# The 32x32 blocks of a delta rule's inversion, taken to one matrix per partition on chip instead of through DRAM

## The chip, the cores and the metric

The kernel runs on one core of a Trainium2 chip. The metric is the device time of one execution in microseconds, smaller is better. Three executions were timed, and one more was recorded by the hardware profiler; its trace and its page are what this document reads.

## The reference, cut to what matters

The kernel computes one decoder layer for a sequence of 1024 tokens and a model width of 1024: a normalised input projection, two mixing branches (an RWKV-7 branch and an S5 branch), gates that merge them, an output projection and a convolutional feed-forward part. The change lies in the RWKV-7 branch, whose core is a scan with a state `S` of 64x64 for each of 8 heads:

```python
def wkv7_scan(r, decay, k, v, a_vec, b_vec):
    ...
    def step(S, inp):
        r_t, w_t, k_t, v_t, a_t, b_t = inp
        sa = jnp.einsum('bhij,bhj->bhi', S, a_t)
        S = (S * w_t[:, :, None, :] + sa[..., None] * b_t[:, :, None, :]
             + v_t[..., None] * k_t[:, :, None, :])
        return S, jnp.einsum('bhij,bhj->bhi', S, r_t)
    ...
    _, ys = lax.scan(step, S0, xs)

def rwkv7_branch(p, mu, w0, w2, a0, a2, g2, k_k, k_a, r_k, lnx_w, lnx_b):
    ...
    y = wkv7_scan(rh, decay.reshape(hs), kh, vh, -kk, kk * ah)
    ...

# the merge: sigmoid(gA)*A + sigmoid(gB)*B, then one output projection
```

The kernel doesn't run this step by step. It takes chunks of 64 tokens. Within a chunk the term `sa` of a token depends on the tokens ahead of it through a strictly triangular 64x64 matrix, so a chunk needs the inverse of one unit triangular matrix per head. This inverse is what the change is about.

## The kernel before, in words

The sequence is worked in two halves of 512 tokens (`th` 0 and 1), each of 8 chunks. The 8 heads lie in two groups (`g`), each of two pairs (`u`) of two heads (`h`). For a half the steps are:

1. **Front** (`rwkv_front`): decays, scaled keys and the products of a group. At its end stand the gram matrices (L716 on PE, L720 masks them on DVE into `gr`), and a product for the bonus term (L724 into `pb`, L736 on DVE with `v`).
2. **Inversion** (`rwkv_inv`): each 64x64 triangular matrix is seen as two 32x32 diagonal blocks and one block beside them. For a half there are 2 groups x 2 blocks x 2 pairs x 8 chunks x 2 heads = 128 diagonal blocks. They are brought to one block per partition, so that one DVE instruction works on all of them, and 30 steps of two tensor_tensor instructions (L789 the product, L791 the sum) build the inverses. In the kernel before, the blocks go there through DRAM: L729 (eight DMAs a half, issued by POOL) writes them from `gr` to `md`, L777 reads `md` into `mt`, one block per partition. Afterwards L793 writes the inverses to `xd`, and eight DMAs at L798 bring them back into `gr`. The identity from which the inverse starts is written by two POOL memsets. A copy of one element (L783) from a result of `rwkv_nat` into the inverse's row 0 makes the inversion begin only after the transposes of nat.
3. **Nat** (`rwkv_nat`, L747): PE transposes of the keys, copied out by ACT (L754, L756, L767).
4. **Level** (`rwkv_level`): the block beside the diagonal, from the two inverses. DVE transposes the first diagonal block (L812), then come two rounds of 64 matmuls of 32x32 (L822 is the first) with ACT copies after each.
5. **Chain** (`rwkv_chain`): the eight chunks one after another, each in three steps (PE L879, ACT copy; PE L887, DVE copy L890; PE L902, DVE L903 and L904).
6. **Out** (`rwkv_out`): normalisation, bonus and gate.

These steps are small and depend on each other. PE's time between them is filled with large matrix products ("fill"): the input projection, the tiles of the two gates (`gate_tiles`, ACT L1158 takes each out of the PSUM tile `gm` and stores it), and then `merge`: gates of the first branch and GLU tiles, gates of the second branch (DVE L1203 multiplies a gate from DRAM with the PSUM tile), and the output projection. The tile `gm` has two slots in this part of the program, and the ring `ev`, into which gates are loaded, has three. A fill tile of 128x512 is a row of k-steps, each of three matmuls (L172, L173, L174) since every operand is split in a high and a low part; L156 (ACT) and L157 (DVE) split the weights, L226 and L227 the activations.

PE's order is written by the program itself: `drive` takes steps from lanes (two preparation lanes, the chain lane, the out lane) and one k-step of fill (`background`) whenever no lane is due. A lane says how long its step takes and how long it is to be left alone afterwards; T_MT, T_INV and T_INV2 are such numbers, for the time from the grams to nat and from nat to the level in the first and the second half. They decide how many k-steps of fill stand between two steps. The orders on DVE, ACT, POOL and SP are made by a scheduler from priorities (the inversion and the weights have the same high one, `HPW`), and each engine then runs its own order strictly.

Of the kernel before, what the change touches and what calls it, by code (L numbers as in the profile page):

```python
# [9 lines left out]
F32 = mybir.dt.float32  # L10
# [3 lines left out]
ALU = mybir.AluOpType  # L14
# [52 lines left out]
class Kern:  # L67
# [564 lines left out]
    def rwkv_tiles(self, d, g, th):  # L632
        pool = self.rk if g else self.rka
        d["ar"] = self.tg("ar", 1, (128, 2, 8, 128), pool=pool)
        d["bk"] = self.tg(f"bk{g}", 1, (128, 2, 8, 128), pool=self.rka)
        d["gr"] = self.tg("gr", 1, (128, 2, 8, 2, 128), pool=pool)
        d["V"] = self.tg(f"V{g}", 1, (128, 8, 2, 64))
        d["md"] = self.md[th][g]
        d["bv"] = self.dram.tile([2, 128, 512], F32, tag="bv", name=self.nm("bv"), bufs=3)

    def rwkv_front(self, d, g, th, pt, start):
# [3 lines left out]
        o = slice(th * 512, th * 512 + 512)  # L645
# [10 lines left out]
        for u in range(2):  # L656
            p = 2 * g + u
# [51 lines left out]
        for u, e in enumerate(L):  # L709
# [13 lines left out]
                    f["pb"] = self.rp()  # L723
                    mm(f["pb"], self.rkb[:, f["p"]], f["r"], start=True, stop=True)  # L724
# [34 lines left out]
    def nat_v(self, d, u, pv):  # L759
# [5 lines left out]
        for k, sl in enumerate(HALF):  # L765
            for h in range(2):
                self.nc.scalar.copy(to[HALF[1 - h], :, k], ps[sl, :, h])  # L767

    def rwkv_inv(self, ds, th):

        nc, V = self.nc, self.nc.vector
        mx = self.tg("mt", 1, (128, 2, 1024))
        mt, x = mx[:, 0], mx[:, 1]
        with self.tc.high_priority(HPW):
            nc.gpsimd.memset(x, 0.0)
            nc.gpsimd.memset(x[:, 0:1024:33], 1.0)
            nc.gpsimd.dma_start(mt, self.md[th].rearrange("g b e q t -> (g b e) (q t)"))  # L777
        yield 0, T_MT
        tie = self.rwkv_nat(ds[1], 1)
        yield 2.0, 0  # L780
        with self.tc.high_priority(HPW):
            mt, x2 = (t.rearrange("p (q t) -> p q t", t=32) for t in (mt, x))
            self.nc.scalar.copy(x2[:, 0, 1:2], tie[:, 0, 0:1])  # L783
            V.tensor_copy(x2[:, 0, 1:32], mt[:, 0, 1:32])
            for q in range(1, 31):
                n, m = q + 1, 31 - q
                tm = self.tg("tm", 1, (128, 256), pool=self.rka)
                tv = tm[:, :n * m].rearrange("p (s t) -> p s t", t=m)
                V.tensor_tensor(tv, x2[:, 0:n, q:q + 1].to_broadcast([128, n, m]),  # L789
                                mt[:, q:q + 1, q + 1:32].to_broadcast([128, n, m]), ALU.mult)  # L790
                V.tensor_tensor(x2[:, 0:n, q + 1:32], x2[:, 0:n, q + 1:32], tv, ALU.add)  # L791
            xds = self.dram.tile([2, 2, 32, 32, 32], F32, tag="xd", name=self.nm("xd"), bufs=2)
            nc.gpsimd.dma_start(xds.rearrange("g b e s t -> (g b e) (s t)"), x)  # L793
            for g, d in enumerate(ds):
                for blk in range(2):
                    for h in range(2):
                        o = 64 * h + 32 * blk
                        nc.gpsimd.dma_start(d["gr"][o:o + 32, :, :, h, 32 * blk:32 * blk + 32].rearrange("p u c t -> p (u c) t"),  # L798
                                            xds[g, blk].rearrange("(e h) s t -> h s e t", h=2)[h])

    def rwkv_level(self, ds):

# [1013 lines left out]
    def front_half(self):  # L1816
# [31 lines left out]
        with tc.tile_pool(name="rk", bufs=1) as self.rk, tc.tile_pool(name="evb", bufs=NEV) as self.evp, \  # L1848
                tc.tile_pool(name="psy", bufs=1, space=PSUM) as self.psx:
            self.ps, self.ngm = self.psx, 2  # L1850
            self.rwkv_setup()
            self.wfp = self.rk
            self.ds = [[{}, {}], [{}, {}]]
            self.grams = 0
            self.fronts, self.masked, self.preps, self.chains, self.chunks, self.outs, self.z = 0, 0, 0, 0, 0, 0, {}
            self.md = [self.dram.tile([2, 2, 32, 32, 32], F32, name=f"md{th}") for th in range(2)]
# [151 lines left out]
```

## Time and profile before

| | us |
|---|---|
| three timed executions | 1474.89, 1477.7, 1479.7 (median 1477.7) |
| the profiled execution | 1475.75 |
| its span in the trace | 1474.0 |
| idle time of PE from 480 to 640 us | 13.7 in all |
| the inversion's steps, first half | 351.04 to 376.86 |
| the inversion's steps, second half | 548.08 to 591.76 |

The mean granted clock of PE over this execution was 0.987. How to read the profile: PE, DVE, ACT and POOL are the tensor, vector, scalar and general engines, PEld is PE's weight load and SP the engine that issues most DMAs. A wait "PE gm L172 <- ACT ev L1158" is idle time of PE ahead of a matmul of line 172 that writes the tile `gm`, ended by an instruction of line 1158 on ACT that writes `ev`. A window's row gives busy time for each engine, and the clock that PE was granted, 1.00 being full speed. The DMAs that the change touches, with their size and the median time from issue to landing in us:

```profile
md<-gr POOLq DMA_DIRECT2D x16, 64.0 KB, 4.6
mt<-md POOLq DMA_DIRECT2D x2, 512.0 KB, 4.0
xd<-mt POOLq DMA_DIRECT2D x2, 512.0 KB, 5.2
gr<-xd POOLq DMA_DIRECT2D x16, 64.0 KB, 3.8
```

### The profile page before, as it was taken

The page shows a single profiled execution, that of the slowest core. Times are in us where ns is not written, and L with a number is a line of the kernel's source. Part 1 is how long each engine was busy: PE and PEld are TensorE (multiplying, and loading weights), DVE is VectorE, ACT ScalarE, POOL GpSimd, SP SyncE. Part 2 cuts the span into 40 slices and gives each one's busy share as a digit, 9 for nine tenths or more (in the row PEclk, how much of TensorE's full clock was granted, in tenths as well). Part 3 has the DMA queues.
Part 4 walks back from the last instruction along what each step waited for, and adds up shares of the span by engine and source line. Part 5 has one row for each costly group of instructions (what it writes and reads, how often), then busy time and mean ns, then how long its engine had stood idle before and what let it go on. Part 6 is the DMA issues. An engine that isn't in the chain of part 4 may idle for free. (4 is left out here: it accounts for less than half of the span.)

```text
span 1474.0 us, 24155 instructions
## 1 busy us (share of the span) xinstructions
PE 1420.3 (96%) x9284; PEld 1161.8 (79%) x9284; DVE 1072.4 (73%) x1761; ACT 729.6 (50%) x1167; POOL 58.9 (4%) x116
## 2 busy tenths in 40 slices
PE   7999999999999999899999999999999999999996
PEld 5778888788877777677788877888888887888775
DVE  8977775665425859657698798777777777697677
ACT  7677654443334653634455454444444544444441
POOL 0000000011100110100000000000000000000001
PEclk9999999999999999899999999999999999999998
DMA  6453433643511575633474543222222227934723
GB/s 219 116 194 120 134 96 88 206 123 117 171 62 63 170 238 164 187 124 108 142 223 145 192 136 112 82 86 86 86 86 86 73 71 256 341 123 140 243 75 114
DMA packets 121284, 206.26 MB, mean 140 GB/s; under 512 B 29248, under 2 KB 35520, under 8 KB 121168
## 3 DMA queue, kind: packets, MB, share of 16 engines
q1 hardware_dynamic: 113296, 182.43, 39.3%
q0 software_dynamic: 6144, 19.99, 4.0%
q10 hardware_dynamic: 1728, 2.29, 0.4%
q8 instruction: 73, 1.20, 0.3%
q14 instruction: 43, 0.35, 0.1%
HBM read 150.14 MB, written 52.43 MB: 137 GB/s over the span
## 5 line engine op out<-in xcount | busy, mean ns | idle before, releaser
L172 PE MATMUL gm<-hh,wh 128*128 128x512 f32 x672 | 276.4, 411 | 9.4 <-DVE ev L1203 4.1
L173 PE MATMUL gm<-hl,wh 128*128 128x512 f32 x672 | 264.8, 394 | 0.1
L174 PE MATMUL gm<-hh,wl 128*128 128x512 f32 x672 | 264.5, 394 | 0.0
L156 ACT CAST wh<-wf 128x512 fp32r<-128x512 f32 x171 | 105.7, 619 | 167.4 <-PE gm L173 99.5
L157 DVE TENSOR_TENSOR wl<-wf,wh 128x512 fp32r<-128x512 f32 x171 | 117.3, 688 | 75.7 <-ACT wh L156 75.1
L172 PEld LDWEIGHTS gm<-hh,wh 128*128 128x128 f32 x672 | 127.5, 190 | 42.1 <-issue 6.0
L174 PEld LDWEIGHTS gm<-hh,wl 128*128 128x128 f32 x672 | 127.6, 190 | 28.0
L173 PEld LDWEIGHTS gm<-hl,wh 128*128 128x128 f32 x672 | 127.8, 190 | 24.7 <-issue 1.0
L1626 PE MATMUL d<-xl,wh 128*128 128x512 f32 x308 | 120.2, 390 | 2.8 <-DVE xl L227 2.8
L1625 PE MATMUL d<-xh,wh 128*128 128x512 f32 x308 | 120.1, 390 | 2.1 <-ACT xh L226 2.1
L1627 PE MATMUL d<-xh,wl 128*128 128x512 f32 x308 | 119.9, 389 | 0.0
L1451 PE MATMUL rp<-t,h 128*128 128x512 f32 x216 | 84.4, 391 | 1.9 <-ACT p L1465 1.9
L1453 PE MATMUL rp<-t,l 128*128 128x512 f32 x216 | 84.2, 390 | 0.5 <-DVE l L227 0.5
L1452 PE MATMUL rp<-t,h 128*128 128x512 f32 x216 | 84.1, 389 | 0.0
L1626 PEld LDWEIGHTS d<-xl,wh 128*128 128x128 f32 x308 | 57.8, 188 | 15.6 <-DVE xl L227 3.9
L1625 PEld LDWEIGHTS d<-xh,wh 128*128 128x128 f32 x308 | 57.8, 188 | 14.5 <-ACT xh L226 2.4
L1627 PEld LDWEIGHTS d<-xh,wl 128*128 128x128 f32 x308 | 57.8, 188 | 12.0
L226 ACT CAST h<-r 128x1024 fp32r<-128x1024 f32 x34 | 35.8, 1054 | 61.1 <-PE rp L1452 29.6
L227 DVE TENSOR_TENSOR l<-r,h 128x1024 fp32r<-128x1024 f32 x34 | 41.7, 1225 | 29.3 <-ACT h L226 27.7
L1472 DVE SCALAR_TENSOR_TENSOR y<-zv,vecs,y 128x1023 f32<-128x1023 f32 (+1 forms) x36 | 46.1, 1281 | 8.5 <-ACT y L1470 8.5
L1451 PEld LDWEIGHTS rp<-t,h 128*128 128x128 f32 x216 | 40.5, 188 | 11.3 <-ACT p L1465 2.7
L1465 ACT COPY p<-rp 128x512 f32<-128x512 f32 x54 | 31.0, 574 | 36.6 <-PE rp L1453 36.6
(459 smaller groups left out, 3163.7 us busy)
## 6 DMA issues: line engine op xcount, KB each, us to landing
r<-in_w_up_dram SPq DMA_DIRECT2D x36, 512.0 KB, 3.7
wf<-in_w_in_dram SPq DMA_DIRECT2D x62, 256.0 KB, 3.1
st<-in_w_down_dram SPq DMA_DIRECT2D x55, 256.0 KB, 4.1
st<-ACT SPq DMA_DIRECT2D x44, 256.0 KB, 4.3
wf<-in_w_up_dram SPq DMA_DIRECT2D x36, 256.0 KB, 2.9
ACT<-y POOLq DMA_DIRECT2D x18, 512.0 KB, 2.9
GT<-ev SPq DMA_DIRECT2D x32, 256.0 KB, 2.5
wf<-in_w_br_dram SPq DMA_DIRECT2D x32, 256.0 KB, 2.9
```

The costliest lines, as they stand in the source:

```text
L156: nc.scalar.copy(h[:, :n], f[:, :n])
L157: nc.vector.tensor_tensor(l[:, :n], f[:, :n], h[:, :n].bitcast(F32), ALU.subtract)
L172: mm(ps, a, xh[k], start=k == 0, stop=False)
L173: mm(ps, a, xl[k], start=False, stop=False)
L174: mm(ps, b, xh[k], start=False, stop=k == n - 1)
L1451: mm(ps, wh[:, c], xh, start=first and k == 0, stop=False, skip_group_check=True)
L1452: mm(ps, wh[:, c], xl, start=False, stop=False, skip_group_check=True)
L1453: mm(ps, wl[:, c], xh, start=False, stop=k == 3, skip_group_check=True)
L1472: V.scalar_tensor_tensor(y[:, lag:], z[:, 0:1024 - lag], self.vec(nme, i), y[:, lag:], ALU.mult, ALU.add)
L1625: mm(ps, wh[:, c], xh[:, x], start=start, stop=False, skip_group_check=True)
L1626: mm(ps, wh[:, c], xl[:, x], start=False, stop=False, skip_group_check=True)
L1627: mm(ps, wl[:, c], xh[:, x], start=False, stop=stop, skip_group_check=True)
```

## The change

The blocks don't leave the chip. `diagonal` gathers them by eight copies, four on DVE and four on ACT in turn, from `gr` (each 32 partitions by 16x32 elements) into one tile, in which 32 partitions hold the rows of 32 blocks beside each other. One DVE transpose instruction of 128x32x32 turns this tile so that each partition holds one block (read and written with a step of 32 elements), a copy of 128x1024 makes the second tile from which the inverse is built in place, and a memset sets the diagonal to one. After the 30 steps a second transpose and eight copies go the way back. The element of the steps' row q itself is now taken from the copied matrix, so a step works on q rows instead of q + 1. The copy that tied the inversion to nat is gone. T_MT, T_INV and T_INV2 are smaller.

```diff
@@ rwkv_front
             if u:
-                for blk in range(2):
-                    for h in range(2):
-                        q = 64 * h + 32 * blk
-                        nc.gpsimd.dma_start(d["md"][blk].rearrange("(e h) q t -> h q e t", h=2)[h],
-                                            d["gr"][q:q + 32, :, :, h, 32 * blk:32 * blk + 32].rearrange("p u c t -> p (u c) t"))
                 self.grams += 1
+    def diagonal(self, ds, m, back):
+
+        m = m.rearrange("p (e h t) -> p e h t", h=2, t=32)
+        n = 0
+        for g, d in enumerate(ds):
+            for blk in range(2):
+                for h in range(2):
+                    o, q = 64 * h + 32 * blk, 32 * (2 * g + blk)
+                    x = d["gr"][o:o + 32, :, :, h, 32 * blk:32 * blk + 32].rearrange("p u c t -> p (u c) t")
+                    y = m[q:q + 32, :, h]
+                    (self.nc.scalar.copy if n % 2 else self.nc.vector.tensor_copy)(*((x, y) if back else (y, x)))
+                    n += 1
@@ rwkv_inv
+        m2, x2 = (t.rearrange("p (q t) -> p q t", t=32) for t in (mt, x))
         with self.tc.high_priority(HPW):
-            nc.gpsimd.memset(x, 0.0)
-            nc.gpsimd.memset(x[:, 0:1024:33], 1.0)
-            nc.gpsimd.dma_start(mt, self.md[th].rearrange("g b e q t -> (g b e) (q t)"))
+            self.diagonal(ds, x, False)
+            V.transpose(mt.rearrange("p (q t) -> p t q", t=32), x.rearrange("p (e t) -> p t e", t=32))
+            V.tensor_copy(x, mt)
+            V.memset(x[:, 0:1024:33], 1.0)
         yield 0, T_MT
-        tie = self.rwkv_nat(ds[1], 1)
+        self.rwkv_nat(ds[1], 1)
         yield 2.0, 0
         with self.tc.high_priority(HPW):
-            mt, x2 = (t.rearrange("p (q t) -> p q t", t=32) for t in (mt, x))
-            self.nc.scalar.copy(x2[:, 0, 1:2], tie[:, 0, 0:1])
-            V.tensor_copy(x2[:, 0, 1:32], mt[:, 0, 1:32])
             for q in range(1, 31):
-                n, m = q + 1, 31 - q
+                m = 31 - q
                 tm = self.tg("tm", 1, (128, 256), pool=self.rka)
-                tv = tm[:, :n * m].rearrange("p (s t) -> p s t", t=m)
-                V.tensor_tensor(tv, x2[:, 0:n, q:q + 1].to_broadcast([128, n, m]),
-                                mt[:, q:q + 1, q + 1:32].to_broadcast([128, n, m]), ALU.mult)
-                V.tensor_tensor(x2[:, 0:n, q + 1:32], x2[:, 0:n, q + 1:32], tv, ALU.add)
-            xds = self.dram.tile([2, 2, 32, 32, 32], F32, tag="xd", name=self.nm("xd"), bufs=2)
-            nc.gpsimd.dma_start(xds.rearrange("g b e s t -> (g b e) (s t)"), x)
-            for g, d in enumerate(ds):
...
+                tv = tm[:, :q * m].rearrange("p (s t) -> p s t", t=m)
+                V.tensor_tensor(tv, x2[:, 0:q, q:q + 1].to_broadcast([128, q, m]),
+                                m2[:, q:q + 1, q + 1:32].to_broadcast([128, q, m]), ALU.mult)
+                V.tensor_tensor(x2[:, 0:q, q + 1:32], x2[:, 0:q, q + 1:32], tv, ALU.add)
+            V.transpose(mt.rearrange("p (e t) -> p t e", t=32), x.rearrange("p (q t) -> p t q", t=32))
+            self.diagonal(ds, mt, True)
-T_KN, T_BK, T_GR, T_NF, T_MT, T_INV, T_LV, T_CH = 7.0, 4.0, 4.0, 5.0, 8.0, 43.0, 1.0, 0.8
-T_LN, T_LE, T_INV2 = 32.0, 16.0, 50.0
+T_KN, T_BK, T_GR, T_NF, T_MT, T_INV, T_LV, T_CH = 7.0, 4.0, 4.0, 5.0, 3.0, 34.0, 1.0, 0.8
+T_LN, T_LE, T_INV2 = 32.0, 16.0, 46.0
```

New line numbers of the changed kernel, where rows below name them: L719 is the gram mask (L720 before), L730 the product with `pb` (L736 before), L773 the copies of `diagonal`, L784 and L798 the two transposes, L785 the copy, L786 the memset, L795 and L797 the steps of the inversion (L789 and L791 before). Lines from 812 on have the same numbers in both.

On PE both kernels issue the same 6359 instructions of their order; only places change. Counted in k-steps of fill that stand ahead of a step:

| step on PE | before | changed |
|---|---|---|
| first half: nat of the second group | 307 | 300 |
| first half: level begins (L762) | 371 | 350 |
| first half: chain begins (L879) | 381 | 360 |
| second half: second group's front (L682) | 434 | 413 |
| second half: last gram (L716) and L724 | 482 | 461 |
| second half: nat of the second group | 502 | 474 |
| second half: level (L762 to L822) | 576 to 582 | 542 to 548 |
| second half: chain | 586 to 632 | 552 to 598 |
| second half: out (L935) | 658 to 673 | 624 to 639 |

From k-step 700 on, the two orders are the same. The fill itself is the same in both: gate tiles to k-step 504, merge's first-branch gates and GLU tiles to 552, second-branch gates from 552 to 584, second half's GLU tiles to 600, gates again to 632, output projection after that.

The first place is DVE in the second half, from the mask of the last gram to the inversion's first steps. Names are tiles with a number: `gr` the grams, `mt` the matrices one per partition, `ld` and `rp` the product of L736. Before:

```order
L720 TENSOR_TENSOR gr_5254<-cz_5699,csts 128x4x128
L736 TENSOR_TENSOR ld_5355<-rp_5718,ld_5523 128x512
L736 TENSOR_TENSOR ld_5358<-rp_5720,ld_5526 128x512
L227 TENSOR_TENSOR hl_5971<-ld_5958,hh_5970 128x512
L227 TENSOR_TENSOR hl_5975<-ld_5960,hh_5974 128x512
L157 TENSOR_TENSOR wl_5982<-wf_5983,wh_5981 128x512
L157 TENSOR_TENSOR wl_6021<-wf_6022,wh_6020 128x512
L157 TENSOR_TENSOR wl_6060<-wf_6061,wh_6059 128x512
L227 TENSOR_TENSOR hl_6006<-hh_6001,hh_6005 128x512
L227 TENSOR_TENSOR hl_6014<-hh_6009,hh_6013 128x512
L784 COPY mt_5758<-mt_5758 128x31
```

In the changed kernel:

```order
L719 TENSOR_TENSOR gr_5162<-cz_5591,csts 128x4x128
L773 COPY mt_5646<-gr_5162 32x16x32 x2
L730 TENSOR_TENSOR ld_5247<-rp_5610,ld_5431 128x512
L784 STREAM_TRANSPOSE mt_5646<-mt_5646 128x32x32
L730 TENSOR_TENSOR ld_5250<-rp_5612,ld_5434 128x512
L785 COPY mt_5646<-mt_5646 128x1024
L795 TENSOR_TENSOR tm_5750<-mt_5646 128x30
L786 MEMSET mt_5646 128x32
L797 TENSOR_TENSOR mt_5646<-mt_5646,tm_5750 128x30
```

The inversion begins directly after the grams, ahead of the splits of merge's first inputs (L227) and weights (L157). The second place is ACT in the second half, around the gate tiles' last activations. Before:

```order
L1158 ACTIVATE ev_5780<-gm_5747,hb_b_gate 128x512
L156 CAST wh_6059<-wf_6061 128x512
L226 CAST hh_6005<-hh_6001 128x512
L226 CAST hh_6013<-hh_6009 128x512
L754 COPY bk_905_5253<-cz_5802 128x4x64
L756 COPY bk_905_5253<-cz_5802 64x4x64 x2
L754 COPY bk_905_5253<-cz_5803 128x4x64
L767 COPY V_907_5255<-rp_5806 64x4x64 x4
L783 COPY mt_5758<-rp_5806 128x1
```

In the changed kernel, where `gr<-mt` are the copies back of the second half:

```order
L1158 ACTIVATE ev_5923<-gm_5898,hb_b_gate 128x512
L773 COPY gr_4813<-mt_5646 32x16x32
L156 CAST wh_6051<-wf_6053 128x512
L773 COPY gr_4813<-mt_5646 32x16x32
L773 COPY gr_5162<-mt_5646 32x16x32 x2
L226 CAST hh_5997<-hh_5993 128x512
L156 CAST wh_6072<-wf_6074 128x512
L1158 ACTIVATE ev_5951<-gm_5926,hb_b_gate 128x512
```

The copies back stand between the last two activations of the gate tiles, where nat's copies stood before. The third place is DVE at the level's transposes in the second half. Before:

```order
L1203 SCALAR_TENSOR_TENSOR ev_6457<-ev_6457,gm_6465 128x512
L227 TENSOR_TENSOR hl_6454<-ld_6450,hh_6453 128x512
L157 TENSOR_TENSOR wl_6900<-wf_6901,wh_6899 128x512
L1249 TENSOR_TENSOR ev_6457<-ev_6457,hl_6203 128x512
L812 STREAM_TRANSPOSE ld_6487<-gr_4905 32x512 x2
L232 SCALAR_TENSOR_TENSOR hl_6502<-ev_6457,hh_6501 128x512
L1203 SCALAR_TENSOR_TENSOR ev_6513<-ev_6513,gm_6521 128x512
L227 TENSOR_TENSOR hl_6510<-ld_6506,hh_6509 128x512
L1249 TENSOR_TENSOR ev_6513<-ev_6513,hl_6252 128x512
L812 STREAM_TRANSPOSE ld_6488<-gr_5254 32x512 x2
```

In the changed kernel:

```order
L812 STREAM_TRANSPOSE ld_6241<-gr_4813 32x512
L157 TENSOR_TENSOR wl_6586<-wf_6587,wh_6585 128x512
L1188 SCALAR_TENSOR_TENSOR ev_6218<-ev_6218,hh_6040 128x512
L812 STREAM_TRANSPOSE ld_6241<-gr_4813 32x512
L812 STREAM_TRANSPOSE ld_6242<-gr_5162 32x512
L232 SCALAR_TENSOR_TENSOR hl_6262<-ev_6218,hh_6261 128x512
L157 TENSOR_TENSOR wl_6667<-wf_6668,wh_6666 128x512
L1203 SCALAR_TENSOR_TENSOR hl_6265<-ev_6266,gm_6274 128x512
L812 STREAM_TRANSPOSE ld_6242<-gr_5162 32x512
```

The level's transposes stand among merge's first GLU tiles and gates now (L1188, L232), and no longer among the second-branch gates (L1203 with L1249).

More of the change, by code (lines that the diff above doesn't have):

```diff
@@ L769, in rwkv_inv @@
     def rwkv_inv(self, ds, th):
-        nc, V = self.nc, self.nc.vector
+        V = self.nc.vector
         mx = self.tg("mt", 1, (128, 2, 1024))
         mt, x = mx[:, 0], mx[:, 1]
+        m2, x2 = (t.rearrange("p (q t) -> p q t", t=32) for t in (mt, x))
         with self.tc.high_priority(HPW):
-            nc.gpsimd.memset(x, 0.0)
-            nc.gpsimd.memset(x[:, 0:1024:33], 1.0)
-            nc.gpsimd.dma_start(mt, self.md[th].rearrange("g b e q t -> (g b e) (q t)"))
+            self.diagonal(ds, x, False)
+            V.transpose(mt.rearrange("p (q t) -> p t q", t=32), x.rearrange("p (e t) -> p t e", t=32))
+            V.tensor_copy(x, mt)
+            V.memset(x[:, 0:1024:33], 1.0)
@@ L778, in rwkv_inv @@
         yield 0, T_MT
-        tie = self.rwkv_nat(ds[1], 1)
+        self.rwkv_nat(ds[1], 1)
         yield 2.0, 0
         with self.tc.high_priority(HPW):
-            mt, x2 = (t.rearrange("p (q t) -> p q t", t=32) for t in (mt, x))
-            self.nc.scalar.copy(x2[:, 0, 1:2], tie[:, 0, 0:1])
-            V.tensor_copy(x2[:, 0, 1:32], mt[:, 0, 1:32])
             for q in range(1, 31):
-                n, m = q + 1, 31 - q
+                m = 31 - q
                 tm = self.tg("tm", 1, (128, 256), pool=self.rka)
-                tv = tm[:, :n * m].rearrange("p (s t) -> p s t", t=m)
-                V.tensor_tensor(tv, x2[:, 0:n, q:q + 1].to_broadcast([128, n, m]),
-                                mt[:, q:q + 1, q + 1:32].to_broadcast([128, n, m]), ALU.mult)
-                V.tensor_tensor(x2[:, 0:n, q + 1:32], x2[:, 0:n, q + 1:32], tv, ALU.add)
-            xds = self.dram.tile([2, 2, 32, 32, 32], F32, tag="xd", name=self.nm("xd"), bufs=2)
-            nc.gpsimd.dma_start(xds.rearrange("g b e s t -> (g b e) (s t)"), x)
-            for g, d in enumerate(ds):
[L795 to L799, printed above, removed]
@@ L1855, in front_half @@
             self.fronts, self.masked, self.preps, self.chains, self.chunks, self.outs, self.z = 0, 0, 0, 0, 0, 0, {}
-            self.md = [self.dram.tile([2, 2, 32, 32, 32], F32, name=f"md{th}") for th in range(2)]
             self.pts = [self.tg("pt", 2, (128, 8, 4)) for th in range(2)]
```

1 line of the change is left out of this document (removed).

## The prediction

> **What bounds the kernel now.** I read the engine totals first, then the windows of the stretch that the change touches, then PE's waits in it.
>
> ```profile
> PE 1420.3 (96%) x9284; PEld 1161.8 (79%) x9284; DVE 1072.4 (73%) x1761; ACT 729.6 (50%) x1167; POOL 58.9 (4%) x116
> ```
>
> PE is busy for 1420.3 of 1474.0 us, and the change takes nothing from it: its instructions are the same, in another order. So the time can only move by idle time of PE, and by time that PE spends at a lower clock. Both halves of the sequence go through the inversion. The windows' columns are us, then the busy time of PE, PEld, DVE, ACT and POOL, the granted clock, the DMA share and GB/s:
>
> ```profile
> 340.00:360.00 20.00, 20.00 (x101) 16.82 (x100) 8.86 (x25) 9.84 (x23) 0.57 (x1) 1.00 0.35 112
> 360.00:380.00 20.00, 20.00 (x90) 16.57 (x89) 16.21 (x44) 4.40 (x8) 0.55 (x1) 1.00 0.31 93
> 380.00:400.00 20.00, 20.00 (x231) 16.69 (x231) 5.74 (x9) 7.41 (x17) 5.19 (x8) 1.00 0.61 193
> 520.00:540.00 20.00, 18.52 (x135) 14.22 (x135) 10.84 (x17) 8.26 (x11) 4.86 (x8) 1.00 0.85 263
> 540.00:560.00 20.00, 18.86 (x93) 15.51 (x92) 14.90 (x35) 15.72 (x34) 0.57 (x1) 1.00 0.56 175
> 560.00:580.00 20.00, 19.27 (x85) 15.46 (x85) 19.65 (x44) 8.20 (x14) 0.00 (x0) 1.00 0.57 168
> 600.00:604.00 4.00, 4.00 (x15) 3.21 (x15) 1.73 (x3) 1.89 (x5) 2.88 (x5) 0.67 0.91 193
> 612.00:616.00 4.00, 1.64 (x52) 1.53 (x54) 3.25 (x6) 2.08 (x6) 0.00 (x0) 0.61 0.80 251
> 616.00:620.00 4.00, 4.00 (x58) 2.90 (x54) 0.55 (x1) 1.81 (x5) 0.00 (x0) 0.54 0.07 26
> ```
>
> In the first half (its inversion ends in the row 360:380, its level is in 380:400) PE is never idle, at full clock: the round trip through DRAM costs nothing there. In the second half there are gaps. PE's waits between 480 and 640 us (total, times, longest) are nearly all of them:
>
> ```profile
> PE gm L172 <- DVE ev L1203: 4.1, 2, 3.1
> PE gm L172 <- ACT ev L1158: 2.6, 2, 1.5
> PE rp L702 <- ACT ld L937: 2.2, 1, 2.2
> PE rp L822 <- ACT hh L231: 2.0, 1, 2.0
> PE gm L172 <- DVE hl L1203: 0.7, 1, 0.7
> PE rp L682 <- DVE ld L736: 0.7, 1, 0.7
> PE cz L822 <- DVE ld L812: 0.4, 1, 0.4
> PE cz L879 <- DVE S L904: 0.4, 1, 0.4
> PE rp L822 <- DVE ld L812: 0.4, 1, 0.4
> PE cz L822 <- ACT hh L231: 0.2, 1, 0.2
> ```
>
> They fall into three places. **Front** (L682, L702): 2.9 us, ahead of the changed code; I cost it at no change. **Merge start** (L172 behind the gate tile's L1158, and the first L1203): 2.6 + 0.7 = 3.3 us. **Level** (L172 behind L1203 of the second-branch gates, and L822): 4.1 + 2.0 + 0.4 + 0.4 + 0.2 = 7.1 us. After the last the clock is down: 4.00 x 0.33 + 1.64 x 0.39 + 4.00 x 0.46 = 3.8 us of PE's busy time are lost in the three short rows, so the level costs 10.9 us. DVE is full in 560:580 (19.65 of 20): the inversion's steps are shuffled among merge's element-wise work.
>
> **First half.** The change removes nine DMA instructions ahead of the inversion and nine behind it, the copy that ties its start to nat, and 465 of 5,425 elements in each of the two products of its steps. Rows of the inversion's end, of the level, and of nat:
>
> ```profile
> 376.64 0.22 DVE L791 TENSOR_TENSOR mt<-mt,tm 128x31 f32<-128x31 f32 x1
> 395.52 2.90 DVE L812 STREAM_TRANSPOSE ld<-gr 32x512 f32<-32x512 f32 x4 [0.26 <-ACT ld L810]
> 346.87 1.03 PE L747 MATMUL cz<-csts,bk 128*128 128x128 f32 x8
> 348.18 1.04 PE L747 MATMUL cz<-csts,bk 128*128 128x128 f32 x8
> 528.00 0.40 PE L172 MATMUL gm<-hh,wh 128*128 128x512 f32 x1
> 528.69 0.39 PE L172 MATMUL gm<-hh,wh 128*128 128x512 f32 x1
> ```
>
> The order has PE's level 21 k-steps earlier (371 to 350) and the start of the chain as many. A k-step of three matmuls takes 0.69 us (528.00 to 528.69; 0.68 below), so this is 14 us, less than the 18.7 us that the way through DRAM and the tiles beside it took from 376.86 to the level at 395.52. On POOL's queue the nine issues each way go, and what stays there, the stores of bv, has nothing new ahead of it; SP's queue is not touched. Fill covers PE throughout and the fill is the same in sum. I put this half at 0; if its cover broke, the level would show it as an L822 wait of the second half's kind, up to 3 us.
>
> **Second half, merge start.** The order puts the whole inversion 21 to 34 k-steps earlier against the fill, so that it lies beside the last gate tiles, and the four ACT copies back (L773) stand on ACT ahead of the L1158 that frees the PSUM slot for merge's first tile. That is a new wait, so I work out both ends of it from the end of the last gram mask:
>
> ```profile
> 526.58 1.28 DVE L720 TENSOR_TENSOR gr<-cz,csts 128x512 f32<-128x512 f32 x2
> 525.48 1.98 PE L724 MATMUL rp<-ld,rkb 128*128 128x512 f32 x4
> L789 DVE TENSOR_TENSOR tm<-mt 128x60 f32<-128x60 f32 (+15 forms) x30 | 10.4, 347 | 1.0
> L791 DVE TENSOR_TENSOR mt<-mt,tm 128x60 f32<-128x60 f32 (+15 forms) x30 | 10.4, 348 | 1.0
> L791 DVE TENSOR_TENSOR mt<-mt,tm 128x255 f32<-128x255 f32 x2 | 0.8, 424 | 0.1
> L1101 DVE TENSOR_SCALAR ev<-ev 128x512 f32<-128x512 f32 x2 | 0.8, 414 | 0.9 <-ACT ev L1100 0.9
> L570 DVE TENSOR_SCALAR t<-t 128x1024 f32<-128x1024 f32 x4 | 2.8, 694 | 6.0 <-ACT t L569 6.0
> L812 DVE STREAM_TRANSPOSE ld<-gr 32x512 f32<-32x512 f32 x8 | 5.6, 700 | 0.4 <-ACT ld L810 0.3
> L1025 ACT COPY ev<-ev 128x512 f32<-128x512 f32 x8 | 9.7, 1213 | 1.8 <-DMA US<-ev 1.0 <-DVE ev L1024 0.6
> L1117 ACT COPY ev<-gm 128x512 f32<-128x512 f32 x8 | 4.7, 583 | 0.7 <-PE gm L174 0.7
> L157 DVE TENSOR_TENSOR wl<-wf,wh 128x512 fp32r<-128x512 f32 x171 | 117.3, 688 | 75.7 <-ACT wh L156 75.1
> L1158 ACT ACTIVATE ev<-gm,hb_b_gate 128x512 f32<-128x512 f32 x32 | 21.9, 684 | 47.2 <-issue 30.9 <-PE gm L174 16.0
> ```
>
> - Copies on DVE: 0.41 us each (L1101 has 512 elements, as they do), and the 1024-element copy L785 0.69 (L570).
> - The transposes of 128x32x32 are in no row of before. L812 moves 512 elements in 0.70 us with elements side by side; the steps' rows give 0.91 ns for each further element (424 ns for 255, 220 for 31), so 1024 take 1.2 us, the lower end. L784 and L798 step 32 elements from one to the next, though. The nearest row with a step is the ACT copy L1025 (steps of 8 elements), 1213 against 583 ns for L1117: 2.1 times. That gives 2.5 us, the upper end. I take the upper: L1025 is the only row with a step between elements.
>
> [...]
>
> - Steps of the inversion in the first half, with the idle time ahead of them: 10.4 + 10.4 + 1.0 + 1.0 = 22.8 us; less 2 x 465 elements at 0.91 ns, 0.8 us: 22.0. The order has eight other operations of 0.69 among them: 27.5.
> - DVE from 527.9: two copies, two L730 (0.69 each), L784 and L785: 527.9 + 0.8 + 1.4 + 1.2 + 0.7 = 532.0, or 533.3 with the slow transpose; the inversion to 559.5 or 560.8; L798 to 560.7 or 563.3. Then ACT: four copies at 0.58, three casts (L156, L226) at the same and L1158 at 0.68: 4.7 us, to 565.4 or 568.0; I take 0.5 off, since a first cast can run while DVE still transposes: 564.9 or 567.5.
> - PE: from the gram's end, 527.5, the order has 13 k-steps, the transposes of nat (2.3 us in the first half, 346.87 to 349.22) and 34 k-steps to the tile that needs the slot (504 to 508 of merge's first): 47 x 0.68 + 2.3 = 34.3, at 561.8.
>
> PE waits 3.1 or 5.7 us, and the first L1203 keeps its 0.7. A clock drop after it costs nothing if the gap is like the 1.5 and 1.1 us here, whose rows (520 to 560) stay at 1.00, or half of the 3.8 us above, 1.9, after a long one. So 3.8 or 8.3 us in place of 3.3: **+0.5 or +5.0**.
>
> **Second half, level and chain.** The order takes the level from k-step 576 to 542 and the chain from 586-632 to 552-598. The level leaves the second-branch gates for merge's lighter part, so the 4.1 us behind L1203 and the 2.0 us behind ACT's L231 have no place there. What comes in is DVE's row: five 0.69 us operations stand among the four L812, 3.4 + 2.8 = 6.2 us against some 4.4 us of fill between: 1.8 us. The chain now lies beside the second-branch gates. It did so in part before (600 to 632) with the one wait of 0.4; at worst it waits 1.2 us in each of 8 chunks, 9.8 (worked out with the second rival). I take 2.0, nearer to that row. A clock drop after the level takes 0 to 3.8; I take 1.5, one window of about 4 us at 0.61. Together 1.8 + 2.0 + 1.5 = 5.3 for 10.9: **-5.6** (bounds: -9.1 with no chain wait and no drop, +4.5 with the worst of both).
>
> [...]
>
> From k-step 700 the order is the same again; I cost that at 0.
>
> **Sum.** 0 + (+5.0 or +0.5) - 5.6: -0.6 with the slow transposes, -5.1 with the fast ones. I take a value a little under the slow one, since the fast end also lowers the clock drop: -1.5. Against the profiled execution's 1475.75 us that is 1474.2. The runs' median, 1477.7, lies 2.0 above that execution, which shares the spread (1474.9 to 1479.7); half of it added gives **1475.2**.
>
> **The rivals.**
> - *The transposes are cheap, or ACT's copies get out of the way:* merge start stays at its 3.3 and the level's gain is whole: -5.1, and -6.1 if the clock drop after the level shrinks with it; at -5.3 it is 1471.4 with the same half added. For it: L812's 0.70 at full width. Against it: the strides.
> - *Slower: the chain beside DVE's fullest part.* Each chunk of the chain needs DVE twice (the copy L890, the sums L903 and L904) and ACT once, with about two k-steps (1.4 us) of fill to hide a reply. With two 0.69 us operations ahead, L890's 0.42 ends at 1.8, 0.4 late, and L903 with L904 (0.84) at 2.2, 0.8 late: 1.2 a chunk, 9.8 in all for eight. With the slow merge start that is 5.0 - 10.9 + 1.8 + 9.8 + 1.5 = +7.2, so 1483.9. It decides from two queued operations on; with one it is nothing. For it: DVE at 19.65 of 20. Against it: the single wait of 0.4 us among gates in before.
> - *The waits only change places:* they come from two PSUM slots and three gate buffers, and any order meets them. 0, 1476.7. Against it: the 4.1 and the 2.0 us stand together, at the level, and the first half has none.
>
> **How the numbers follow.** Chances: forecast 0.50 (its own range 1472 to 1479), cheap transposes 0.27, chain 0.15, same waits elsewhere 0.08. A measurement of this kernel can tell about 0.3%, 4.4 us, from no change. Faster by more than that is the second case and a twelfth of the forecast, 0.31; slower is the third and a bit of the forecast's upper edge, 0.17; the rest 0.52. The range takes the two outer cases to their middle: 1468 to 1483.
>
> **What would show it.** L784 and L798 near 2.5 or 1.2 us tell the first two cases apart; an L172 wait behind L1158 of 3 to 6 us at the start of merge tells the ACT block; L822 waits under 2 us tell the level; waits of L902, L887 or L879 add up to the third case above 5 us. No gap may appear in the first half. The forecast is wrong if PE's idle time shrinks by more than 7 us or grows by more than 4 us in this stretch.

## The result, and the profile after

The changed kernel is **slower**: 1494.67 us (median of four runs, 1492.36 to 1498.01) against 1476.3 for the kernel before beside it (four runs); the ratio is 1.0114, 95% interval 1.0089 to 1.0138. The forecast was 1475.2 in a range of 1468 to 1483. The profiled execution has a span of 1490.6 us against 1474.0, so 16.6 us are to be found. PE's waits of the changed kernel from 470 to 700 us (total, times, longest) answer to the list of before:

```profile
PE gm L172 <- ACT ev L1158: 7.5, 2, 7.2
PE gm L172 <- ACT hh L231: 6.6, 1, 6.6
PE cz L879 <- DVE S L904: 6.4, 5, 4.2
PE rp L701 <- ACT ld L937: 2.0, 1, 2.0
PE rp L822 <- DVE ld L812: 1.3, 1, 1.3
PE gm L174 <- DVE wl L157: 1.0, 1, 1.0
PE cz L887 <- ACT p L881: 0.9, 1, 0.9
PE cz L715 <- DVE gr L719: 0.6, 2, 0.4
PE rp L681 <- DVE ld L730: 0.3, 1, 0.3
```

The level's waits of before (4.1 us behind L1203, 2.0 behind L231 ahead of L822) are gone, as forecast. Three long ones took their place, and each is followed by windows at half clock (columns: us, busy PE, PEld, DVE, ACT, POOL, granted clock, DMA share, GB/s):

```profile
552.00:556.00 4.00, 1.07 (x3) 0.88 (x4) 2.29 (x4) 3.96 (x8) 0.00 (x0) 0.50 0.55 189
556.00:560.00 4.00, 4.00 (x11) 3.13 (x10) 2.51 (x5) 0.94 (x2) 0.00 (x0) 0.50 0.69 198
560.00:564.00 4.00, 4.00 (x16) 3.22 (x16) 1.76 (x3) 1.24 (x2) 0.00 (x0) 0.87 0.45 136
624.00:628.00 4.00, 4.00 (x53) 2.85 (x50) 0.34 (x1) 1.14 (x3) 0.00 (x0) 0.50 0.50 135
628.00:632.00 4.00, 4.00 (x100) 3.28 (x93) 3.44 (x7) 2.38 (x4) 0.00 (x0) 0.84 0.39 128
668.00:672.00 4.00, 0.92 (x2) 0.41 (x2) 4.00 (x18) 1.82 (x3) 0.00 (x0) 0.50 0.38 122
672.00:676.00 4.00, 4.00 (x10) 3.13 (x11) 3.93 (x12) 0.62 (x1) 0.00 (x0) 0.50 0.35 106
676.00:680.00 4.00, 4.00 (x17) 3.23 (x16) 1.84 (x3) 0.62 (x1) 0.00 (x0) 0.86 0.41 124
```

At 0.50 the matmuls of a k-step start 0.43 us apart (672.47 to 673.75), at 1.00 they start 0.23 apart (502.05 to 502.97), so I take busy time times the missing share of the clock as lost. That gives 1.07 x 0.50 + 4.00 x 0.50 + 4.00 x 0.13 = 3.1 us after the first, 4.00 x 0.50 + 4.00 x 0.16 = 2.6 after the second, 0.92 x 0.50 + 4.00 x 0.50 + 4.00 x 0.14 = 3.0 after the third. For the front of the second half, which I had costed at no change, the rows are, of before and then of the changed kernel:

```profile
496.00:500.00 4.00, 4.00 (x21) 3.60 (x21) 3.89 (x12) 0.73 (x2) 2.63 (x5) 0.60 0.76 184
500.00:504.00 4.00, 4.00 (x21) 4.00 (x20) 2.13 (x4) 2.94 (x7) 0.00 (x0) 0.55 0.64 196
```

```profile
480.00:484.00 4.00, 3.81 (x25) 3.54 (x26) 4.00 (x7) 2.16 (x4) 1.08 (x2) 0.82 0.40 141
484.00:488.00 4.00, 4.00 (x25) 3.79 (x25) 2.94 (x10) 3.54 (x11) 0.00 (x0) 0.76 0.44 138
```

That is 3.4 us of clock before and 1.6 after. All places, in us; where two numbers stand, the first is the wait and the second the time lost by the clock:

| place | before | forecast | after |
|---|---|---|---|
| first half | 0 | 0 | 0 |
| front of the second half | 2.9 + 3.4 | same | 2.9 + 1.6 |
| merge start | 3.3 | 8.3 | 8.5 + 3.1 |
| level | 7.1 + 3.8 | 1.8 + 1.5 | 1.3 |
| chain | 0.4 | 2.0 | 7.3 + 2.6 |
| out step | 0 | 0 | 6.6 + 3.0 |

The sums are 20.9 before and 36.9 after: 16.0 of the 16.6 us. They are of one execution of each kernel; the clock's part differs between executions, as a later paragraph shows. What follows finds the cause of each of the three new waits.

### The profile page after: what moved, and what is told of

It is laid out like the page before. It is cut to its first block, busy times and chain, and to the rows that moved or that the text cites. A ratio compares the mean times of both kernels' runs of the same rounds, so it can differ in the third digit from the quotient of the medians.

```text
span 1490.6 us, 24115 instructions
## 1 busy us (share of the span) xinstructions
PE 1424.5 (96%) x9284; PEld 1164.8 (78%) x9284; DVE 1087.1 (73%) x1783; ACT 740.9 (50%) x1181; POOL 33.4 (2%) x76
## 5 line engine op out<-in xcount | busy, mean ns | idle before, releaser
L157 DVE TENSOR_TENSOR wl<-wf,wh 128x512 fp32r<-128x512 f32 x171 | 117.3, 688 | 74.7 <-ACT wh L156 73.4
L226 ACT CAST h<-r 128x1024 fp32r<-128x1024 f32 x34 | 35.8, 1054 | 61.1 <-PE rp L1452 29.6
L227 DVE TENSOR_TENSOR l<-r,h 128x1024 fp32r<-128x1024 f32 x34 | 41.6, 1225 | 29.2 <-ACT h L226 27.7
L1465 ACT COPY p<-rp 128x512 f32<-128x512 f32 x54 | 31.0, 574 | 37.1 <-PE rp L1453 36.9
```

Source lines behind the costliest of these rows:

```text
L157: nc.vector.tensor_tensor(l[:, :n], f[:, :n], h[:, :n].bitcast(F32), ALU.subtract)
```

## The experiments

The theory after the result (A): the loss comes from PE's new order, that is from where the smaller T_MT, T_INV and T_INV2 put nat, level, chain and out against the fill, and hardly from the on-chip path. The rival (B): the path itself, with strided transposes of 4.3 us and 16 copies a half on engines that merge needs.

**The two parts of the change apart.** The changed kernel with the old numbers:

```diff
-... T_MT, T_INV, T_LV, T_CH = 7.0, 4.0, 4.0, 5.0, 3.0, 34.0, 1.0, 0.8
-T_LN, T_LE, T_INV2 = 32.0, 16.0, 46.0
+... T_MT, T_INV, T_LV, T_CH = 7.0, 4.0, 4.0, 5.0, 8.0, 43.0, 1.0, 0.8
+T_LN, T_LE, T_INV2 = 32.0, 16.0, 50.0
```

> The on-chip path with the old numbers T_MT, T_INV and T_INV2, so PE's order is that of before. Theory A (the loss comes from where the new numbers put nat, level, chain and out against the fill): no PE wait of 6 to 7 us behind L1158 at merge start, none of 6.6 us behind ACT L231 at the out stage, chain waits under 1 us; 1474 to 1480 us. Theory B (the on-chip path itself costs, 4 us of strided transposes and 16 copies a half on engines that merge needs): the stall at merge start stays near 8 us and the time stays at 1488 or more.

Measured: 1480.76 us, ratio 1.0011 (0.999 to 1.0031), a little above theory A's range; its waits are as A said, 3.3 us at most behind L1158, none at the out step, 0.4 in the chain. The kernel before with only the new numbers (the same two lines the other way round):

> The kernel before with only the three numbers changed, so PE's order is that of the changed kernel and the blocks still go through DRAM. Theory A: the chain's waits (about 7 us and a clock drop) and the wait at the out stage (6.6 us and a clock drop) are there as in the changed kernel, and the level waits for the DRAM trip on top; 1488 us or more. Theory B: these waits are small and the time stays at 1474 to 1480.

Measured: 1495.68 us, ratio 1.0103 (1.0063 to 1.0142). Its waits from 530 to 700 us:

```profile
PE gm L172 <- ACT hh L231: 6.6, 1, 6.6
PE gm L172 <- DVE hl L1203: 6.6, 1, 6.6
PE cz L879 <- DVE S L904: 5.5, 4, 4.0
PE rp L822 <- DVE ld L812: 1.3, 1, 1.3
```

All three new waits are there with the blocks still going through DRAM, the longest of each within 0.6 us. At merge start it is DVE's L1203 that ends the wait, though this kernel has no copies back. So A holds for the loss: the three numbers carry it alone. The on-chip path as the change has it, that is without the tie to nat, shows no difference that these runs can tell; with the tie kept it is not free, as the tied run below shows. One part of my expectation failed: the level does not wait for the DRAM trip even at the earlier place (1.3 us in both).

**Level, chain and out put back, grams left** (`T_INV2 = 69.0` for 46.0 in the changed kernel):

> The changed kernel with T_INV2 69 in place of 46: level, chain and out of the second half stand at the k-steps of before (576, 586 to 632, 658), grams and nat at those of the changed kernel. Theory A: merge start keeps its 8 us and its clock drop (11 us in all), chain and out lose their waits (about 17 us with the clock), the level has a wait of at most 3 to 6 us: 1478 to 1484. Theory B: no change from 1494.7 by more than 3 us.

Measured: 1481.19 us, ratio 1.002 (1.0004 to 1.0036). Merge start keeps 7.3 us; chain (0.4) and out (none) are as before, and the level has 1.0 + 2.8 us ahead of L822 and 2.1 behind L1203. So putting the three back is worth 13.5 us, and what the level's earlier place gained is less than what chain and out lost by theirs.

**The out step alone** (in the out lane, ahead of `rwkv_out`):

```diff
             yield 0, lambda: self.chains > th
+            if th:
+                yield 0, 23.0
```

> The changed kernel with the second half's out step held back by 23 us of the planner's time, so that only its DVE work (L918 to L928) and its tiles move, to the k-steps of before (658 on); level and chain stay at 542 and 552. If that work ahead of the GLU tile's L1188 and L231 is what stalls PE for 6.6 us at k-step 600, this wait and the 3 us of half clock after it go: about 9.6 us less, 1485. If the wait belongs to the GLU tile whatever stands beside it, no change (1492 to 1497).

Measured: 1485.27 us, 9.4 less than the changed kernel; at the place of the 6.6 us, 0.5 and 0.7 are left. The changed kernel's rows there show the queue:

```profile
663.56 1.21 DVE L918 TENSOR_REDUCE lm<-mt 128x16 f32<-128x1024 f32 x1
664.69 1.22 DVE L920 TENSOR_TENSOR mt<-mt,lm 128x1024 f32<-128x1024 f32 x1
666.02 1.22 DVE L920 TENSOR_TENSOR mt<-mt,lm 128x1024 f32<-128x1024 f32 x1
667.17 1.86 DVE L925 TENSOR_REDUCE lv<-ev 128x8 f32<-128x512 f32 x3
669.62 0.68 DVE L1188 SCALAR_TENSOR_TENSOR ev<-ev,ld 128x512 f32<-128x512 f32 x1
670.33 0.63 ACT L231 ACTIVATE hh<-ev 128x512 fp32r<-128x512 f32 x1 [1.11 <-DVE ev L1188]
671.01 0.80 PE L172 MATMUL gm<-hh,wh 128*128 128x512 f32 x1 [6.60 <-ACT hh L231]
```

The chain ends at k-step 598, so the normalisation's long operations enter DVE's order just ahead of the last GLU tile's L1188, whose split (L231) the gates from k-step 600 need. In the kernel before, the chain ended at 632, where the output projection begins, and PE has no wait from 640 to 720 us there.

**The chain.** The changed kernel's rows at its longest chain wait:

```profile
619.57 1.12 ACT L1178 ACTIVATE ld<-ev 128x512 f32<-128x512 f32 x1 [1.87 <-DMA ev<-YU]
620.99 0.62 ACT L226 CAST hh<-ld 128x512 fp32r<-128x512 f32 x1
621.63 0.69 DVE L227 TENSOR_TENSOR hl<-ld,hh 128x512 fp32r<-128x512 f32 x1 [2.10 <-ACT hh L226]
622.55 0.69 DVE L232 SCALAR_TENSOR_TENSOR hl<-ev,hh 128x512 fp32r<-128x512 f32 x1 [0.23 <-ACT hh L231]
623.16 0.42 DVE L904 TENSOR_TENSOR S<-S,pt 128x256 f32<-128x256 f32 x1
623.64 1.13 PE L879 MATMUL cz<-S,ar 64*64 64x64 f32 x32 [4.15 <-DVE S L904]
```

DVE is not full here: it waits for ACT, and ACT for a load of the S5 inputs (YU), which merge brings in beside the second-branch gates. L904 stands behind them. The first try put these loads into the larger ring:

```diff
-        self.ys5.append(self.s5_y(self.ev((128, 8, 64)), b, 1, self.tg("ld", NLD)))
+        self.ys5.append(self.s5_y(self.tg("ld", NLD, (128, 8, 64)), b, 1, self.tg("ld", NLD)))
```

> The changed kernel with the S5 inputs' loads (YU) of the second half in the ring of ten tiles (ld) in place of the ring of three (ev), so that they can start earlier; level, chain and out stay. If the chain's 4.2 us wait for S is DVE's L904 queued behind an L227 that waits for this load, it falls under 1 us and the half clock after it (2.6 us) goes: 5 to 7 us less, about 1489. If DVE is simply full there, the wait moves to another step of the chain: 1493 to 1496.

Measured: 1491.72 us. The wait didn't go, it moved to an earlier chunk (4.79 us), with the same cause:

```profile
602.02 1.12 ACT L1178 ACTIVATE ld<-ld 128x512 f32<-128x512 f32 x1 [3.38 <-DMA ld<-YU]
```

Together with the later out step:

> Both edits. If the two waits are apart, the gains add up: 15 to 17 us less, 1477 to 1480, with merge start's wait of 8 us left. If they share a cause, it is nearer to the larger one alone, 1485.

Measured: 1482.54 us, the out step's gain and little more. Then each load was started two gate tiles ahead of its use, its GELU left where it stood in the program:

```diff
+            if m < 4:
+                yu.append(self.tg("ld", NLD, (128, 8, 64)))
+                nc.sync.dma_start(yu[m], self.YU[m].rearrange("j c g n -> (c g) j n")[:, :, 64:128])
             if 2 <= m < 6:
-                self.s5_inputs(m - 2)
+                self.s5_inputs(m - 2, yu[m - 2])
```

> The changed kernel with each S5 input's load started two gate tiles (10 us) ahead of its use, into the ring of ten; all else stays. If the chain's long wait is ACT's L1178 waiting for that load, with DVE's L227 and L904 behind it, no L879 wait above 1 us is left and the clock drop goes: 6 to 8 us less than the changed kernel, 1487 to 1489. If DVE's own load is the cause, a wait of 4 us stays at some step: 1492 or more.

Measured: median 1490.3 us, span of the profiled execution 1485.8 (1490.6 in the changed kernel). No chain wait above 0.6 us is left from 600 to 665 us:

```profile
PE cz L879 <- DVE S L904: 2.0, 4, 0.6
```

The cause of the long chain wait is settled by the trace. Its price is 4.4 us by the medians, 4.8 by the spans and 6.4 by the ratios (1.0071 against 1.0114), with runs from 1482.9 to 1493.6: at the lower end of the 6 to 8 that I wrote or below it, and under the 9.9 of the table. The clock tells why. The waits from 470 to 770 us fell by 5.7 us (28.7 to 23.0) and the drop after the chain's wait went, but in this execution the level's one wait of 1.3 us is followed by 5.1 us of lost clock (0.50 for 10 us), where the changed kernel's execution lost nothing after the same wait. With the later out step:

> That and the out step held back by 23 us: 9.4 us less again if the two are apart, 1478 to 1480, with only merge start's 8 us and its half clock left of the loss.

Measured: 1479.84 us, ratio 1.0012 (0.9993 to 1.003): with chain and out mended, the changed kernel is level with the one before, and merge start's 7.1 us is the one long wait left.

**Merge start.** All copies back on DVE, so that L1158 has none ahead of it on ACT:

```diff
-(self.nc.scalar.copy if n % 2 else self.nc.vector.tensor_copy)
+(self.nc.scalar.copy if n % 2 and not back else self.nc.vector.tensor_copy)
```

> The changed kernel with the copies back all on DVE, so no instruction of ACT that merge needs stands behind the inversion. If ACT's copies ahead of L1158 are the whole block at merge start, the wait there falls from 8.2 us to under 1.5 us and the time by 7 to 11 us, to about 1485. If DVE itself is late (the weight splits L157 of merge's tiles stand behind the inversion on DVE too), PE only gets on when these are done: the wait falls by 2 to 3 us, to about 5 to 6, and the time to about 1491.

Measured: 1491.39 us; the wait is as long, 8.3 us, behind DVE's L1203 in place of ACT's L1158. The time is that of the second case, the wait of neither: ACT's copies are not the block by themselves. With all eight copies on DVE it holds PE as long; without any copies back, in the run through DRAM above, it still held PE for 6.6 us. The steps of the inversion left out in the second half (`range(1, 1 if th else 31)`):

> The changed kernel without the 30 steps of the second half's inversion (left out; copies and transposes stay). If the inversion's 22 us on DVE ahead of merge's own DVE work are what stalls PE at merge start, the 8.2 us wait goes to under 1 us, with the clock drop: about 11 us less, 1484, chain and out waits staying. If the transposes and the copies do it, 3 us or more of the wait stay: 1487 to 1491.

Measured: 1484.05 us, 10.6 less, and the waits from 510 to 560 us are short:

```profile
PE gm L172 <- ACT ev L1158: 2.4, 4, 1.1
PE gm L172 <- DVE hl L1203: 0.7, 1, 0.7
```

So the block is DVE's stretch of steps (25.8 us in the changed kernel, from 522.2 to 547.95, with eight other operations of 0.69 among them), which stands in its order ahead of merge's first L1203 and of the copies on both engines. Two tries to put the steps among merge's work followed. The tie of before, with the old numbers:

```diff
+            self.nc.scalar.copy(x2[:, 0, 1:2], tie[:, 0, 0:1])
+            V.tensor_copy(x2[:, 0, 1:2], m2[:, 0, 1:2])
```

> The on-chip path with the old numbers (PE's order of before) and the old tie: one element of nat's result is copied into the inversion's tile, so that it begins after nat again, among merge's work on DVE. If merge start's wait comes from the inversion standing whole ahead of merge's DVE work, it is now that of before (3.3 us), against 4.6 without the tie, and with the way back on chip the level's waits are at most those of before (7.1): 1472 to 1478, ratio 0.996 to 1.001. If the strided transposes and copies on DVE and ACT weigh more than the DRAM way they replace, 1480 or more.

Measured: 1488.75 us, ratio 1.0067 (1.0042 to 1.0091). The wait at merge start did fall to 2.85 us, but the steps now end at 589 us and the second-branch gates wait 3.3 and 1.9 us behind L1203 (L1205 in that file) again. This time the way back on chip stands ahead of the gate that PE waits for, 4.4 us of DVE with one L157 among it:

```profile
589.10 2.20 DVE L800 STREAM_TRANSPOSE mt<-mt 128x1024 f32<-128x1024 f32 x1
591.77 1.70 DVE L773 COPY gr<-mt 32x512 f32<-32x512 f32 x4
593.50 0.69 DVE L1205 SCALAR_TENSOR_TENSOR ev<-ev,gm 128x512 f32<-128x512 f32 x1
594.33 0.77 PE L172 MATMUL gm<-hh,wh 128*128 128x512 f32 x1 [3.29 <-DVE ev L1205]
```

In the kernel before, the longest wait behind L1203 (3.1 us) is ended by one that itself waited 1.7 us for its gate's load. So my expectation's second case came true, 1480 or more: with the tie and PE's order of before in both kernels, the on-chip path is 0.7% slower than the one through DRAM, and the 1.0011 of the untied version is the sum of this and of what the missing tie gives back. The rows show the way back as the cause of one of the waits; where the rest of the 0.7% comes from was not tried apart. The level moved forward from there:

> The same with T_INV2 45 in place of 50: level and chain 7 k-steps earlier (569 and 579), using the time that the way through DRAM took. If the level then meets less of the second-branch gates: 2 to 4 us less than the tied one, 1470 to 1475. If the inversion isn't done by then, or the chain gets into the S5 inputs: L822 or L879 waits of 3 us or more and 1480 or above.

Measured: 1486.68 us, ratio 1.0047 (1.0031 to 1.0063); the gates' waits stay. And numbers between the two sets, with the early loads:

> The changed kernel with T_MT 3, T_INV 43, T_INV2 41 and the S5 loads started early: grams 14 k-steps later than in the changed kernel (475), nat at 488, level at 549 to 555, chain 559 to 605. DVE's order then has merge's first L157, L227 and L1203 among the inversion's steps and not behind them. If that was merge start's block, its wait is under 3 us, the level has none above 1.5 us, chain and out none: 1466 to 1474, faster than before. If merge start waits whatever the order, because DVE has 22 us of steps to do within 26 k-steps more: a wait of 5 us or more and 1476 to 1480.

> The same with T_INV2 46: level at 556 to 562, at the first second-branch gates. The same merge start; L822 waits of 1 to 3 us if those gates are what the level waits for: 1 to 4 us more than with 41.

Measured: 1493.41 and 1495.46 us, both as slow as the changed kernel. This theory of mine fell: with merge's work among the steps on DVE, ACT is late instead. At 549 to 555 the level's copies stand behind the S5 GELUs, which the early loads let ACT take sooner, and PE waits 6.1 us for one of them; merge start waits 4.3 us behind L1158 with nat's copies and four GELUs ahead of it, and the out step 4.6.

**Does the path gain anything?** The early loads with the old numbers, on chip and through DRAM:

> The on-chip path with the old numbers and the S5 loads started early and out of the ring of three. If part of the level's waits (L172 behind L1203 of the second-branch gates, 2.7 us) came from that ring, 2 to 4 us less than without the early loads: about 1477. If not, 1480.

> The kernel before with only the S5 loads started early. It says how much of a gain belongs to these loads and not to the on-chip path: if the 4.1 us behind L1203 go, 1473 to 1475; if the level's waits only change places, no change (1476 to 1479). The on-chip path is worth the difference to the run with the old numbers and early loads.

Measured: on chip 1476.7 us, ratio **0.9981** (0.9965 to 0.9998); through DRAM 1482.58 us, ratio 1.002 (1.0006 to 1.0033), beside runs of before at 1480.07. The first is the one version here whose median lies below that of the kernel before in the same session, and barely: its interval ends at 0.9998, and it is one of sixteen versions tried. Against the DRAM path with the same early loads it is clear, 5.9 us by the medians. Part of that is the DRAM version getting worse, which I hadn't expected (1473 to 1479): its waits behind L1203 shrink from 4.8 to 0.6 us, but those behind L1158 grow from 2.6 to 7.7. With DRAM the steps end late and the way back follows them:

```profile
603.99 0.21 DVE L791 TENSOR_TENSOR mt<-mt,tm 128x31 f32<-128x31 f32 x1
604.79 0.56 POOL L793 DMA_DIRECT2D xd<-mt  x1 [62.86 <-DVE ev L1250]
609.06 1.98 POOL L798 DMA_DIRECT2D gr<-xd  x3 [3.71 <-DMA xd<-mt]
```

The level then waits (L822 behind L812, 5.8 + 1.0 us), while on chip the last step is done by 573.6 us and the same waits are 2.1 + 0.2. On chip the steps also begin sooner, since no tie to nat holds them (537.9 us in the version with the old numbers, 548.1 in the kernel before). How the gain divides between the missing tie and the shorter way wasn't tried apart with the early loads. Without them the untied version is 0.6% faster than the tied one, and the tied one 0.7% slower than the way through DRAM, so there it is the missing tie that gains.

## Why the prediction was wrong, point by point

- **First half, 0:** right. PE has no wait above 0.6 us from 300 to 470 us in the changed kernel.
- **The transposes:** right, and the choice between the bounds too:

```profile
L784 DVE STREAM_TRANSPOSE mt<-mt 128x1024 f32<-128x1024 f32 x2 | 4.4, 2219 | 0.0
L798 DVE STREAM_TRANSPOSE mt<-mt 128x1024 f32<-128x1024 f32 x2 | 4.2, 2092 | 0.1
```

  2.2 and 2.1 us against the 2.5 taken and the 1.2 estimated for neighbouring elements. (L1025 was not the only row with a step, as the prediction has it: ACT's L1178 writes with a step of 8 as well, 1.1 to 1.3 us for 512 elements, against 0.68 for L1158's activation of as many without one, though of another function.)
- **Merge start, +5.0:** the place and the sign were right, the size too small by 3.3 us and the reason half right. The wait was 8.5 us for 6.4 and the clock lost 3.1 for 1.9. My working started when the last gram is made; but the mask of that gram began late, behind an operation of the first half's out step that waited for its load:

```profile
513.58 0.69 DVE L945 TENSOR_TENSOR ld<-ld,ld 128x512 f32<-128x512 f32 x1 [3.67 <-DMA ld<-bv]
547.99 1.96 DVE L798 STREAM_TRANSPOSE mt<-mt 128x1024 f32<-128x1024 f32 x1
549.98 0.61 ACT L773 COPY gr<-mt 32x512 f32<-32x512 f32 x1 [10.72 <-DVE mt L798]
554.19 0.68 ACT L1158 ACTIVATE ev<-gm,hb_b_gate 128x512 f32<-128x512 f32 x1
554.93 0.80 PE L172 MATMUL gm<-hh,wh 128*128 128x512 f32 x1 [7.21 <-ACT ev L1158]
```

  The masks ended 5.7 us after PE's last gram work (517.3 against 511.6) and not 0.4. From there on the work on DVE and ACT ran 2 us faster than worked out (37.6 for 39.6 us to PE's start behind L1158), and PE itself came 1.8 us later (36.1 us after its gram work for 34.3). And I named ACT's copies as the block, where DVE holds PE for 6.6 us with no copies back at all.
- **Level and chain, -5.6:** wrong. The level did what was forecast (1.3 us for 1.8). That it had no clock drop is luck of the one execution: eight more of the versions above have the level at this place with the same wait (1.3 us, 1.6 in one of them), and in their executions 1.6 to 1.7 us of clock are lost there in six, 5.1 and 6.8 in two; the 1.5 that I allowed is the right size. The chain is the term that failed, 2.0 us forecast for 9.9 (7.3 of wait, 2.6 of clock). It was put at 2.0 because "it did so in part before (600 to 632) with the one wait of 0.4". That row is from the gates behind the S5 inputs' loads. In the new place the chain runs beside these loads, and a wait of ACT for DRAM (1.87 us) goes through L226, L227 and L904 to PE (4.15 us). My rival for the chain had the right place and the wrong mechanism: it counted busy operations ahead of L904, where a waiting one stood.
- **From k-step 700 the same, at 0:** this hid the step that failed most. I costed what lies beyond the chain by where the two orders meet again and never the out step between, though it moves by 34 k-steps too, with 10 us of DVE work at its head (L918 to L928). It cost 9.6 us, and putting it back gave 9.4. Between the forecast's sum for the profiled execution, -0.6, and the 16.0 of the table the out step makes 9.6 us of the difference, the chain 7.5 and merge start 3.3; the level and the front took 3.8 back.
- **The clock:** each of the three waits brought its own drop of 2.6 to 3.1 us. I had allowed 1.9 for one and 1.5 for another, and each of the three is above both. Long waits cost about one and a half times their length here (18.0 us in the three waits of 7.2, 4.2 and 6.6, 8.7 in clock behind them).
- **The rival that the waits only change places:** its time, no change, is what the path gives with the old numbers (ratio 1.0011), but not its mechanism: the level's waits, which went, had cost 10.9 us with the clock, and the three that came or grew cost 31.1. And I had not separated the path from its numbers. That split was in the diff, and forecasting the two apart would have set the risk of the order apart from that of the path.

The median of the tied version is 8 us above that of the untied one, where the profiled spans are only 3.9 apart (1484.1 and 1480.2). The traces account for most of it: from 470 to 770 us the tied one has 4 us more of waits (21 and 17) and 3.0 more of lost clock (10.3 and 7.3), while outside this stretch the untied execution happened to lose 4.6 us more to the clock. What stays open: why the level's 1.3 us wait is followed by no lost clock in one execution and by 6.8 us in another, and which of ACT's groups at merge start would have to move for the numbers in between to pay.

## What to carry to other kernels

When a change shortens a side path and planning numbers follow it, forecast the two apart: here the path changed the time by something between 0.7% for the worse (with the tie kept) and 0.4% for the better (untied, both kernels with early loads), and the numbers cost about 1%. Follow everything that moves with the numbers to its end, and ask of each new neighbour not how busy it keeps an engine but what it *waits* for, since here a wait of ACT for DRAM (1.87 us) was handed on to what stood behind it, and PE waited 4.15 us. And DVE, whose order around a 25.8 us block was almost free of gaps (busy for 30.1 of 32 us from 520 to 552), had no slack, however its mean load looked (73%): PE waited 7.2 us.

## What the runs showed of the hardware

A DVE transpose of 128x1024 with a step of 32 elements on both sides takes 2.09 us (L798) and 2.22 us (L784) in the mean, about 1.8 times the 1.2 us estimated for neighbouring elements, which no run has. The copies of 32 partitions by 512 elements take 0.42 us on DVE and 0.62 on ACT, nearly as long as operations on 128 partitions by 512 (0.41 for L1101, 0.58 for L1117). A long wait of PE in these traces (7.2, 4.2 and 6.6 us) is followed by 2.6 to 3.1 us of lost clock; the level's wait of 1.3 us was followed by anything from none (the changed kernel) to 6.8 (the new numbers with DRAM).
